# Logarithm and exponential from one named activation table; block inverses with their products in turn at different array positions

## The chip, the cores and the metric

The kernel runs on one core of one Trainium2 chip. A core has five engines that take their instructions from queues of their own: PE (TensorE, the matrix engine), DVE (VectorE), ACT (ScalarE), POOL (GpSimd) and SP (SyncE, which here only starts transfers). They meet through semaphores. PE has a clock that a throttle grants; in the rows it stands at 1.2 GHz (granted clock 0.50) or 2.4 GHz (1.00). The metric is the device time of one execution in microseconds, lower is better: 3612.3 us, the median of three runs (3611.49, 3612.3, 3624.09).

## What is computed

One inference step of a two-layer model over 128 context tokens and 1024 latent tokens of width 1024. Layer 0 mixes tokens by bidirectional gated linear attention (GLA) with pooling, layer 1 by a bidirectional gated delta rule with 8 heads, and each layer ends with a gated feed-forward network with a width-3 convolution. What the change touches, cut from the reference:

```python
def _layernorm(x, g, b):
    ...
    return ((xf - mu) * lax.rsqrt(var + EPS) * g + b)
def _delta_chunk(q, k, v, g, beta, s0):
    ...
    ld = exp(where(incl, b[..., :, None] - b[..., None, :], -inf))
    kk = where(strict, einsum('bhnid,bhnjd->bhnij', kb, k) * ld, 0.0)
    t = triangular_solve(eye + kk, eye, lower=True, unit_diagonal=True)
    u = einsum('bhnij,bhnjv->bhniv', t, v * beta[..., None])
    ...
    def step(s, xs):          # one chunk after the other
        v_new = u_c - w_c @ s
        o = q_c @ s + a_c @ v_new
        s = s * d_c + k_c.T @ v_new
```

So every head needs the inverse of a unit triangular matrix for every chunk, in both directions, before its scan over the chunks can start. Logarithms and exponentials come from the gates (log-sigmoid, softplus, decays) and from every reciprocal square root, which the kernel computes as exp(-0.5 ln x).

## The kernel before, in words

All 1152 tokens stay on the chip in 9 tiles of 128, or 3 chunks of 384 columns. The three-pass products (`L306` to `L308`: high by high, low by high, high by low) are the bulk of PE's work: projections and feed-forward. Other work of PE is laid between them by generators: a line `yield` ends a slot, and `tick` lets the next generator in a list go on by one slot. The order of the instructions is thus fixed when the program is written out; on the chip each engine runs its list in that order.

The activation tables. ACT evaluates Ln, Exp, Silu, Sqrt and others from a table that has to be loaded (`ACT_TABLE_LOAD`). Before the change nothing in the kernel names one; the compiler puts a load ahead of each activation whose function isn't in the table that it takes to be loaded, and it takes Ln and Exp from two different tables. So the reciprocal square root (`rsqrt`, `L315` Ln and `L316` Exp) has a load ahead of each of its two activations. It is used by the layer norms (`lnr<-psvar`) and by the GLA output's norm (`ss`). The GLA gates (`L1063`, `L1064`), the delta heads' preparation (`L1462` Ln of the key norms, `L1466` Exp) and the delta gates (`L1400` to `L1403`) alternate in the same way.

The delta stage. Heads run one after the other. Head h's scan has 9 steps of 3 slots, 27 slots: `L1690` (key by state), `L1706` (query by state) with `L1708` (inverse by residual, reads the tile U), `L1716` (state update) with `L1727` (output). A scan step is a chain of PE, DVE and ACT, so between a scan's slots PE runs one slot of other work: a slot of the output projection (`parts`: three-pass products `L306` to `L308`, or a transpose and two products at `L827`), of the finishing of the head before (`fin`), and of the next head's inverse (`inv`), which begins at slot `ILAG` = 7 and is run for h < 7. Head 0's own inverse runs ahead of its scan, by itself.

The inverse (`inverse`, from `L1605`). The 32 by 32 blocks on the diagonal have been inverted earlier by substitution, in a batch over all heads, and lie in memory as `yd`. For each head and direction the kernel loads them in quarters into T (`T<-yd`, transposed pairs) and U (`U<-yd`), beside the matrix N itself (`Nl<-Nd`). The other blocks follow by products: for each of two directions and two pairs of blocks, XS = N block by T block (`L1615`), U block = -(XS by U block) (`L1625`), and for one pair in each direction a T block = -(U by XS) (`L1632`): ten products of 32 by 32 blocks, each 9 matmuls (one per tile of 128) that all stand at the same position in the PE array. Then the same with 64 by 64 blocks: XH = N by T (`L1643`) and U block = -(XH by U) (`L1653`), eight groups of 5 or 4 matmuls. Each product writes one bank of PSUM, and ACT brings it to SBUF (`L1617` copy, `L1627` and `L1634` times -1). Each product is a slot: 18 slots, at slots 7 to 24 of the scan of the head before.

Banks of PSUM. In the delta stage four banks are in the pool that `self.ps()` takes from in turn, for all but the scan itself (which has pk0, pk1, po0, po1): the three-pass products, the transposes at `L827` and the inverse share them.

Loads. SP issues all transfers of this stage from one list, in the order in which the slots ask for them: `Nl`, then T, then U, `vt`, `ktok`, between the scan's `qka` tiles. Each issue sits behind the issue before it.

Of the kernel before, what the change touches and what calls it, by code (L numbers as in the profile page):

```python
# [19 lines left out]
T = TC + TL  # L20
# [235 lines left out]
class Kern:  # L256
    def __init__(self, tc, I, O):
        self.tc, self.nc, self.I, self.O = tc, tc.nc, I, O
        self.bg, self.side, self.sums = [], [], {}
        self.pe = ExitStack()  # L260

        self.pace = 0

# [45 lines left out]

    def rsqrt(self, out, in_, scale, tmp=None):  # L310
# [4 lines left out]
        nc.scalar.activation(t, in_, AF.Ln, bias=self.eps[:n], scale=scale)  # L315
        nc.scalar.activation(out, t, AF.Exp, scale=-0.5)  # L316
# [64 lines left out]
    def consts(self):  # L381
# [7 lines left out]
        nc.scalar.activation(self.sc32[:, :, 0:2], self.cc, AF.Silu)  # L389
# [267 lines left out]
    def ffn(self, l, lnp, last, order):  # L657
# [21 lines left out]
        def gate(f, t, raws, dst):  # L679

            n = 1153
            for i in (1, 0):
# [6 lines left out]
                if i:  # L689
                    nc.scalar.activation(t[1], t[1], AF.Silu)  # L690
# [21 lines left out]
        def gate_t(c, f, pss, t, hh, hl):  # L712
# [4 lines left out]
            for i in (1, 0):  # L717
# [11 lines left out]
                if i:  # L729
                    nc.scalar.activation(t[1], t[1], AF.Silu)  # L730
# [205 lines left out]
    def in_proj0(self, p, vp):  # L936
# [9 lines left out]
        with L("pool0") as pp:  # L946
# [16 lines left out]
            with L("rgate") as rp:  # L963
                rt = {}
    
                def evac_r(b, c, ps):
# [4 lines left out]
                    if c == NC - 1:  # L971
                        nc.scalar.activation(rt[b], rt[b], AF.Silu)
# [62 lines left out]
    def gla_a(self, hb, p):  # L1035
# [47 lines left out]
        for d in range(2):  # L1083
# [4 lines left out]
            nc.scalar.activation(x, b, AF.Exp)  # L1088
            nc.vector.tensor_tensor(tiles(y), last.to_broadcast([128, NT, 128]), tiles(b), op=ALU.subtract)
            nc.scalar.activation(y, y, AF.Exp)  # L1090
# [19 lines left out]
        def decays(s):  # L1110
# [10 lines left out]
            nc.scalar.activation(e, e, AF.Exp)  # L1121
# [254 lines left out]
    def silu(self, out, x):  # L1376
        self.nc.scalar.activation(out, x, AF.Silu)
# [7 lines left out]
    def gates_body(self, p):  # L1385
# [14 lines left out]
        nc.scalar.activation(l, l, AF.Exp, scale=-1.0)  # L1400
        nc.scalar.activation(l, l, AF.Ln, bias=1.0)
        al = p.tile([128, 16], F32, name="al")
        nc.scalar.activation(al, self.v("a_log"), AF.Exp)  # L1403
# [14 lines left out]
        nc.scalar.activation(self.negeb, self.b, AF.Exp)  # L1418
        nc.vector.tensor_scalar(self.negeb, self.negeb, -1.0, None, op0=ALU.mult)
        ptv = pt[:, :NT * 16].rearrange("p (n h) -> p n h", h=16)  # L1420
        nc.scalar.activation(self.dec, ptv, AF.Exp)
# [14 lines left out]
    def delta_a(self, h, qT, kT, tp):  # L1436
# [25 lines left out]
        nc.scalar.activation(ss, ss, AF.Ln, bias=self.eps)  # L1462
# [3 lines left out]
        nc.scalar.activation(kl, ss, AF.Exp, scale=0.5)  # L1466
# [4 lines left out]
        nc.scalar.activation(rho, rho, AF.Exp)  # L1471

        flat = lambda t: t.rearrange("p n i -> p (n i)")
        for d, t in ((0, Nt[1]), (1, At[1])):
            x = flat(t)
            nc.scalar.activation(x, bc[:, d], AF.Exp)  # L1476
# [6 lines left out]
        for d in range(2):  # L1483
            c = 8 * d + h
            for n in range(NT):
                e = bc[:, d, n * 128:n * 128 + 128]
                nc.vector.scalar_tensor_tensor(e, e, self.b[:, n, c:c + 1], self.v("msk_b" if d else "msk_f"), op0=ALU.subtract, op1=ALU.min)  # L1487
                nc.scalar.activation(e, e, AF.Exp, bias=lrho[:, d, n:n + 1])
# [116 lines left out]
    def inverse(self, N, Us, T64, tp):  # L1605
# [345 lines left out]
```

## Time and profile before

| | us |
|---|---|
| median of three runs | 3612.3 (3611.49, 3612.3, 3624.09) |
| the profiled execution | 3613.56 |
| its span (first to last instruction) | 3611.7 |
| PE busy | 3278.3 (91%) |
| DVE busy | 2264.6 (63%) |
| POOL busy | 1189.1 (33%) |
| ACT busy | 1145.0 (32%) |
| delta heads, first scan to end of the last | 2203.5 to 2607.6 |

The span is what the profile resolves; 1.9 us of the profiled execution lie around it. A busy share is a mean over stages. PE is busy in nearly all of the feed-forward stages; in the delta stage it is filled by the slots described above; it stands still at the ends of stages, where a norm or a gate has to be finished first. What ended last is read from the chain of waits, which goes back from the last instruction to what released each one.

### The profile page before, as it was taken

The page shows a single profiled execution, that of the slowest core. Times are in us where ns is not written, and L with a number is a line of the kernel's source. Part 1 is how long each engine was busy: PE and PEld are TensorE (multiplying, and loading weights), DVE is VectorE, ACT ScalarE, POOL GpSimd, SP SyncE. Part 2 cuts the span into 40 slices and gives each one's busy share as a digit, 9 for nine tenths or more (in the row PEclk, how much of TensorE's full clock was granted, in tenths as well). Part 3 has the DMA queues.
Part 4 walks back from the last instruction along what each step waited for, and adds up shares of the span by engine and source line. Part 5 has one row for each costly group of instructions (what it writes and reads, how often), then busy time and mean ns, then how long its engine had stood idle before and what let it go on. Part 6 is the DMA issues. An engine that isn't in the chain of part 4 may idle for free.

```text
span 3611.7 us, 54689 instructions
## 1 busy us (share of the span) xinstructions
PE 3278.3 (91%) x21774; PEld 3050.6 (84%) x21774; DVE 2264.6 (63%) x3749; ACT 1145.0 (32%) x2334; POOL 1189.1 (33%) x768
## 2 busy tenths in 40 slices
PE   6988898999999999789789899899969999999887
PEld 4877677899999989688778888799858999999886
DVE  4386465656665677664577774655646667576766
ACT  2434323511111111455343432455563111111133
POOL 1221136322222325543223330344533232222454
PEclk9989878999999999889889997899979999999998
DMA  6212544122222112214544647554401111111232
GB/s 253 93 60 77 166 142 135 67 91 100 88 94 82 47 40 84 82 59 137 165 150 154 198 145 222 161 152 152 135 18 40 37 47 42 41 42 41 65 99 93
DMA packets 248877, 370.18 MB, mean 102 GB/s; under 512 B 67647, under 2 KB 185695, under 8 KB 248240
## 3 DMA queue, kind: packets, MB, share of 16 engines
q1 hardware_dynamic: 240612, 349.54, 30.2%
q10 hardware_dynamic: 7340, 14.92, 1.2%
q8 instruction: 173, 2.83, 0.3%
q0 software_dynamic: 672, 2.23, 0.2%
q14 instruction: 80, 0.66, 0.1%
HBM read 284.69 MB, written 81.93 MB: 102 GB/s over the span
## 4 chain that ended last, share of the span: by engine, by line
PE 66%; DVE 17%; ACT 7%; DMA 5%; issue 2%; SPq 1%; POOL 1%; ACTq 0%; DVEq 0%; POOLq 0%
PE ps L306 18%; PE ps L307 17%; PE ps L308 17%; DVE bc L1487 2%; DVE S L513 2%; DVE lns L522 2%; PE psm L419 1%; DVE lnt L572 1%; DVE S L584 1%; DVE cv L728 1%; DMA bc<-brow 1%; ACT UH L612 1%; ACT lnt L614 1%; PE po L1727 1%; PE pk L1716 1%
## 5 line engine op out<-in xcount | busy, mean ns | idle before, releaser
L306 PE MATMUL ps<-UH,whi 128*128 128x384 f32 (+1 forms) x3408 | 1212.0, 356 | 9.3 <-ACT UH L612 7.3
L307 PE MATMUL ps<-UL,whi 128*128 128x384 f32 (+1 forms) x3408 | 1174.6, 345 | 33.6 <-POOL UL L589 23.9
L308 PE MATMUL ps<-UH,wlo 128*128 128x384 f32 (+1 forms) x3408 | 1170.9, 344 | 3.9 <-POOL wlo L245 3.9
L513 DVE SCALAR_TENSOR_TENSOR S<-ps,mod,S 128x384 f32<-128x384 f32 (+1 forms) x1376 | 603.4, 507 | 479.1 <-PE ps L308 478.8
L244 POOL TENSOR_SCALAR whi<-raw 128x1024 fp32r<-128x1024 f32 x262 | 306.9, 1171 | 1705.6 <-PE ps L307 1164.1
L306 PEld LDWEIGHTS ps<-UH,whi 128*128 128x128 f32 x3408 | 659.8, 194 | 63.8 <-issue 43.8
L307 PEld LDWEIGHTS ps<-UL,whi 128*128 128x128 f32 x3408 | 660.9, 194 | 44.0 <-POOL UL L589 26.9
L245 POOL TENSOR_TENSOR wlo<-raw,whi 128x1024 fp32r<-128x1024 f32 x262 | 660.4, 2521 | 21.9
L308 PEld LDWEIGHTS ps<-UH,wlo 128*128 128x128 f32 x3408 | 659.5, 194 | 4.8 <-POOL wlo L245 4.8
L306 PE MATMUL ps<-hh,whi 128*128 128x384 f32 x1056 | 367.1, 348 | 43.0 <-DVE S L513 17.9
L308 PE MATMUL ps<-hh,wlo 128*128 128x384 f32 x1056 | 363.0, 344 | 4.0 <-POOL wlo L245 4.0
L307 PE MATMUL ps<-hl,whi 128*128 128x384 f32 x1056 | 361.0, 342 | 0.3 <-DVE hl L733 0.3
L306 PEld LDWEIGHTS ps<-hh,whi 128*128 128x128 f32 x1056 | 202.7, 192 | 54.6 <-issue 25.8
L690 ACT ACTIVATE cv<-cv 128x1153 f32<-128x1153 f32 x36 | 42.2, 1173 | 616.9 <-DVE cv L687 616.9
L687 DVE SCALAR_TENSOR_TENSOR cv<-raw,vec,cv 128x1153 f32<-128x1153 f32 x136 | 204.6, 1504 | 4.6
L308 PEld LDWEIGHTS ps<-hh,wlo 128*128 128x128 f32 x1056 | 202.8, 192 | 4.6 <-POOL wlo L245 4.6
L307 PEld LDWEIGHTS ps<-hl,whi 128*128 128x128 f32 x1056 | 203.3, 193 | 1.1 <-DVE hl L733 1.1
L651 ACT COPY raw<-ps 128x384 f32<-128x384 f32 (+2 forms) x272 | 94.9, 407 | 344.7 <-PE ps L308 344.7
L516 POOL TENSOR_TENSOR S<-S,gp 128x384 f32<-128x384 f32 x96 | 97.0, 1013 | 173.5 <-ACT gp L511 173.0
L684 DVE TENSOR_SCALAR cv<-raw,vec 128x1153 f32<-128x1153 f32 x68 | 112.8, 1658 | 13.5 <-ACT raw L651 13.5
L728 DVE SCALAR_TENSOR_TENSOR cv<-ps,vec,cv 128x383 f32<-128x383 f32 (+4 forms) x128 | 61.6, 513 | 83.1 <-ACT edge L724 63.3
L1487 DVE SCALAR_TENSOR_TENSOR bc<-bc,bsum,vecd 128x128 f32<-128x128 f32 x144 | 97.6, 746 | 20.3 <-ACT NA L1476 20.3
(316 smaller groups left out, 4239.2 us busy)
## 6 DMA issues: line engine op xcount, KB each, us to landing
raw<-wall SPq DMA_DIRECT2D x260, 512.0 KB
qka<-pack SPq DMA_DIRECT2D x144, 192.0 KB
lnt<-wmod SPq DMA_DIRECT2D x48, 512.0 KB
wm<-wmod SPq DMA_DIRECT2D x40, 512.0 KB
pack<-NA SPq DMA_DIRECT2D x32, 576.0 KB
bc<-brow SPq DMA_DIRECT2D x16, 576.0 KB
Nd<-NA SPq DMA_DIRECT2D x16, 576.0 KB
pack<-cv SPq DMA_DIRECT2D x16, 512.0 KB
```

The lines of the kernel that those rows point to most:

```text
L244: nc.gpsimd.tensor_scalar(hi, raw, 1.0, 0.0, op0=ALU.mult, op1=ALU.add)
L245: nc.gpsimd.tensor_tensor(lo, raw, hi.bitcast(F32), op=ALU.subtract)
L306: mm(out, wh, uh, start=first, stop=False)
L307: mm(out, wh, ul, start=False, stop=False)
L308: mm(out, wl, uh, start=False, stop=last)
L513: nc.vector.scalar_tensor_tensor(d, ps[:, lo - c * CW:hi - c * CW], g, d, op0=ALU.mult, op1=ALU.add)
L516: nc.gpsimd.tensor_tensor(d, d, t, op=ALU.add)
L651: nc.scalar.copy(raw[:, d:d + hi - lo], ps[:, lo - c * CW:hi - c * CW])
L684: nc.vector.tensor_scalar(t[i], raws[i][:, 0:n], w[:, 0:1], None, op0=ALU.mult)
L687: nc.vector.scalar_tensor_tensor(t[i], raws[i][:, k:n + k], w[:, k:k + 1], t[i], op0=ALU.mult, op1=ALU.add)
L728: nc.vector.scalar_tensor_tensor(t[i][:, a:b], ps[:, a + o:b + o], w[:, k:k + 1], t[i][:, a:b], op0=ALU.mult, op1=ALU.add)
L1487: nc.vector.scalar_tensor_tensor(e, e, self.b[:, n, c:c + 1], self.v("msk_b" if d else "msk_f"), op0=ALU.subtract, op1=ALU.min)
```

## The change

Two things. First, a method `act` replaces `nc.scalar.activation` wherever the function is Ln, Exp, Silu or Sqrt. It keeps the name of the table set that it loaded last; if the function belongs to another set, it loads that set by name. Ln and Exp both belong to `natural_log_exp_and_others`. Activations with other functions (copy, square, abs, scaling) are as before. Second, `inverse` computes the same 18 products in 7 bursts: the four XS products together, one matmul of each in turn, at four different array positions, then the four U products, the two T products, and the 64-wide products of the two directions in pairs. Each product still has a bank of its own, so the first two bursts hold four banks at once. The evacuations follow each burst. Behind every burst stand two `yield`s, so a burst is issued at every other slot: slots 7, 9, 11, 13, 15, 17 and 19.

```diff
         self.pace = 0
+        self.tables = None
...
 
+    def act(self, out, in_, func, **k):
+
+        s = {AF.Silu: "silu_and_others", AF.Sqrt: "sqrt_and_others"}.get(func, "natural_log_exp_and_others")
+        if s != self.tables:
+            self.nc.scalar.preload_act_table_set(s)
+            self.tables = s
+        self.nc.scalar.activation(out, in_, func, **k)
+
     def rsqrt(self, out, in_, scale, tmp=None):
 
         nc = self.nc
         t = out if tmp is None else tmp
         n = in_.shape[0]
-        nc.scalar.activation(t, in_, AF.Ln, bias=self.eps[:n], scale=scale)
-        nc.scalar.activation(out, t, AF.Exp, scale=-0.5)
+        self.act(t, in_, AF.Ln, bias=self.eps[:n], scale=scale)
+        self.act(out, t, AF.Exp, scale=-0.5)
...
             x = g[:, n0:n1]
-            nc.scalar.activation(x, x, AF.Exp, scale=-1.0)
-            nc.scalar.activation(x, x, AF.Ln, bias=1.0)
+            self.act(x, x, AF.Exp, scale=-1.0)
+            self.act(x, x, AF.Ln, bias=1.0)
...
-        self.nc.scalar.activation(out, x, AF.Silu)
+        self.act(out, x, AF.Silu)
...
         pairs = [((0, 1), (2, 3)), ((3, 2), (1, 0))]
-        for d in range(2):
-            for a, b in pairs[d]:
-                ps = self.ps()
-                for n in range(NT):
-                    nc.tensor.matmul(ps[qd(b), 32 * n:32 * n + 32], N[d][qd(a), n, qd(b)], T64[d][qd(a), n, 32 * (a % 2):32 * (a % 2) + 32],
-                                     start=True, stop=True, tile_position=(32 * a, 32 * b))
-                nc.scalar.copy(XS[qd(b), d], ps[qd(b), :288].rearrange("p (n c) -> p n c", c=32))
-                yield
-        for i in range(2):
-            for d in range(2):
-                a, b = pairs[d][i]
-                U, Tt = Us[d], T64[d]
-                ps = self.ps()
-                for n in range(NT):
-                    nc.tensor.matmul(ps[qd(a), 32 * n:32 * n + 32], XS[qd(b), d, n], U[qd(b), n, qd(b)],
-                                     start=True, stop=True, tile_position=(32 * b, 32 * a))
-                nc.scalar.mul(U[qd(a), :, qd(b)], ps[qd(a), :288].rearrange("p (n c) -> p n c", c=32), -1.0)
-                yield
-                if i == 0:
-                    ps = self.ps()
-                    for n in range(NT):
-                        nc.tensor.matmul(ps[qd(b), 32 * n:32 * n + 32], U[qd(b), n, qd(b)], XS[qd(b), d, n],
-                                         start=True, stop=True, tile_position=(32 * b, 32 * b))
-                    nc.scalar.mul(Tt[qd(b), :, 32 * (a % 2):32 * (a % 2) + 32], ps[qd(b), :288].rearrange("p (n c) -> p n c", c=32), -1.0)
-                    yield
+        cols = lambda ps, x, n: ps[qd(x), 32 * n:32 * n + 32]
+        all9 = lambda ps, x: ps[qd(x), :288].rearrange("p (n c) -> p n c", c=32)
+        half = lambda T, x: slice(32 * (x % 2), 32 * (x % 2) + 32)
+
+        four = [(d, a, b) for d in range(2) for a, b in pairs[d]]
+        pss = [self.ps() for _ in four]
+        for n in range(NT):
+            for ps, (d, a, b) in zip(pss, four):
+                nc.tensor.matmul(cols(ps, b, n), N[d][qd(a), n, qd(b)], T64[d][qd(a), n, half(T64, a)],
+                                 start=True, stop=True, tile_position=(32 * a, 32 * b))
+        for ps, (d, a, b) in zip(pss, four):
+            nc.scalar.copy(XS[qd(b), d], all9(ps, b))
+        yield
+        yield
+        pss = [self.ps() for _ in four]
+        for n in range(NT):
+            for ps, (d, a, b) in zip(pss, four):
+                nc.tensor.matmul(cols(ps, a, n), XS[qd(b), d, n], Us[d][qd(b), n, qd(b)],
+                                 start=True, stop=True, tile_position=(32 * b, 32 * a))
+        for ps, (d, a, b) in zip(pss, four):
+            nc.scalar.mul(Us[d][qd(a), :, qd(b)], all9(ps, a), -1.0)
+        yield
+        yield
+        two = [(d, *pairs[d][0]) for d in range(2)]
+        pss = [self.ps() for _ in two]
+        for n in range(NT):
+            for ps, (d, a, b) in zip(pss, two):
+                nc.tensor.matmul(cols(ps, b, n), Us[d][qd(b), n, qd(b)], XS[qd(b), d, n],
+                                 start=True, stop=True, tile_position=(32 * b, 32 * b))
+        for ps, (d, a, b) in zip(pss, two):
+            nc.scalar.mul(T64[d][qd(b), :, half(T64, a)], all9(ps, b), -1.0)
+        yield
+        yield
         XH = tp.tile([128, NT, 64], F32, name="XH", tag="XH")
         hf = lambda x: slice(64 * x, 64 * x + 64)
-        for d in range(2):
-            a, b = d, 1 - d
+        for second in range(2):
             for n0, n1 in ((0, 5), (5, 9)):
-                ps = self.ps()
+                pss = [self.ps() for _ in range(2)]
                 for n in range(n0, n1):
-                    nc.tensor.matmul(ps[hf(b), 64 * (n - n0):64 * (n - n0) + 64], N[d][hf(a), n, hf(b)], T64[d][hf(a), n, :],
-                                     start=True, stop=True, tile_position=(64 * a, 64 * b))
-                nc.scalar.copy(XH[hf(b), n0:n1], ps[hf(b), :64 * (n1 - n0)].rearrange("p (n c) -> p n c", c=64))
-                yield
-        for d in range(2):
-            a, b = d, 1 - d
-            U = Us[d]
-            for n0, n1 in ((0, 5), (5, 9)):
-                ps = self.ps()
-                for n in range(n0, n1):
-                    nc.tensor.matmul(ps[hf(a), 64 * (n - n0):64 * (n - n0) + 64], XH[hf(b), n], U[hf(b), n, hf(b)],
-                                     start=True, stop=True, tile_position=(64 * b, 64 * a))
-                nc.scalar.mul(U[hf(a), n0:n1, hf(b)], ps[hf(a), :64 * (n1 - n0)].rearrange("p (n c) -> p n c", c=64), -1.0)
+                    c = slice(64 * (n - n0), 64 * (n - n0) + 64)
+                    for d in range(2):
+                        a, b = d, 1 - d
+                        if second:
+                            nc.tensor.matmul(pss[d][hf(a), c], XH[hf(b), n], Us[d][hf(b), n, hf(b)],
+                                             start=True, stop=True, tile_position=(64 * b, 64 * a))
+                        else:
+                            nc.tensor.matmul(pss[d][hf(b), c], N[d][hf(a), n, hf(b)], T64[d][hf(a), n, :],
+                                             start=True, stop=True, tile_position=(64 * a, 64 * b))
+                for d in range(2):
+                    a, b = d, 1 - d
+                    o = a if second else b
+                    u = pss[d][hf(o), :64 * (n1 - n0)].rearrange("p (n c) -> p n c", c=64)
+                    if second:
+                        nc.scalar.mul(Us[d][hf(a), n0:n1, hf(b)], u, -1.0)
+                    else:
+                        nc.scalar.copy(XH[hf(b), n0:n1], u)
+                yield
                 yield
```

At all other places `nc.scalar.activation(...)` or `self.silu` became `self.act(...)` with the same operands. A line number of before grows by 1 from `L306` on, by 9 behind `act`, by 13 at the start of `inverse` and by 21 behind it; every activation that goes through `act` stands at `L317`, and all table loads that remain at `L315`.

The compiled program has 107 table loads before and 55 after; the rest of ACT's list keeps its order. On ACT, at a layer norm at the end (the squares `lnt`, then the reciprocal square root of the variance; `lnr` is its tile, `psvar` the bank with the variance), before:

```order
L559 ACTIVATE lnt<-S 128x768 [waits DVE_49] x4
L315 ACT_TABLE_LOAD
L315 ACTIVATE lnr<-psvar,eps 128x384 [waits PE_49]
L316 ACT_TABLE_LOAD
L316 ACTIVATE lnr<-lnr 128x384 [waits Activation_49]
```

and after the change, on the same engine at the same place:

```order
L568 ACTIVATE lnt<-S 128x768 [waits DVE_49] x4
L315 ACT_TABLE_LOAD
L317 ACTIVATE lnr<-psvar,eps 128x384 [waits PE_49]
L317 ACTIVATE lnr<-lnr 128x384 [waits Activation_49]
```

The load ahead of the logarithm stands as before; the one between logarithm and exponential is gone.

On PE, in head 3's scan at slots 7 to 9, where the inverse of head 4 begins (T0, T1 and U10, U11 are the tiles T and U of the two directions, ps are banks, the DMAHW names are the lanes on which loads report), before:

```order
L1615 MATMUL ps_20670<-T0_17597,Nl_20513 32x32 [waits DMAHW2_49,DMAHW0_49]
L1615 MATMUL ps_20670<-T0_17597,Nl_20513 32x32 x8
L306 MATMUL ps_20681<-ohi_20049,whi_18690 128x384
L307 MATMUL ps_20681<-olo_20050,whi_18690 128x384
L308 MATMUL ps_20681<-ohi_20049,wlo_18691 128x384
L1716 MATMUL pk_20633<-y_20663,kr_20640 128x128 [waits Activation_49]
L1716 MATMUL pk_20634<-y_20665,kr_20645 128x128 [waits DVE_49,Activation_49]
L1727 MATMUL po_20635<-y_20663,qka_20492 128x128
L1727 MATMUL po_20636<-y_20665,qka_20494 128x128
L1615 MATMUL ps_20702<-T0_17597,Nl_20513 32x32 [waits DMAHW0_49]
L1615 MATMUL ps_20702<-T0_17597,Nl_20513 32x32 x8
```

and after, the first round of the first burst and what follows it up to the first round of the second:

```order
L1628 MATMUL ps_20718<-T0_17644,Nl_20561 32x32 [waits DMAHW2_49,DMAHW0_49]
L1628 MATMUL ps_20719<-T0_17644,Nl_20561 32x32 [waits DMAHW0_49]
L1628 MATMUL ps_20720<-T1_17645,Nl_20562 32x32 [waits DMAHW3_49,DMAHW1_49]
L1628 MATMUL ps_20721<-T1_17645,Nl_20562 32x32 [waits DMAHW1_49,Activation_49]
...
L307 MATMUL ps_20762<-ohi_20152,whi_18782 128x384 [waits Activation_49]
L1737 MATMUL pk_20681<-y_20711,kr_20688 128x128
L307 MATMUL ps_20783<-ohi_20152,whi_18782 128x384 [waits Activation_49]
L1711 MATMUL pk_20790<-Sd_20768,qka_20598 128x128 [waits DMAHW6_49,DVE_49]
L1637 MATMUL ps_20806<-U10_17642,XS_20717 32x32 [waits DMAHW7_49,Activation_49]
L1637 MATMUL ps_20807<-U10_17642,XS_20717 32x32 [waits DMAHW1_49,Activation_49]
L1637 MATMUL ps_20808<-U11_17643,XS_20717 32x32 [waits DMAHW6_49]
L1637 MATMUL ps_20809<-U11_17643,XS_20717 32x32 [waits DMAHW2_49,Activation_49]
```

The waits for the four loads of T, which before stood at slots 7 to 10 (`L1615`), now stand at the head of slot 7; the waits for U, before at slots 11 to 16, stand at slot 9; and the first three-pass product behind each burst of four (`L307` here) waits for ACT to empty a bank, which before it didn't. The order of SP's list of transfers is the same before and after.

## Rows read from the trace of the kernel before

**Rows 1.** The page: span, PE and ACT busy, the chain's shares by engine.
```profile
span 3611.7 us, 54689 instructions
...
PE 3278.3 (91%) x21774; PEld 3050.6 (84%) x21774; DVE 2264.6 (63%) x3749; ACT 1145.0 (32%) x2334; POOL 1189.1 (33%) x768
...
PE 66%; DVE 17%; ACT 7%; DMA 5%; issue 2%; SPq 1%; POOL 1%; ACTq 0%; DVEq 0%; POOLq 0%
```

**Rows 2.** Groups of ACT's instructions: line, count | busy us, mean ns | idle before.
```profile
L316 ACT ACT_TABLE_LOAD x21 | 26.9, 1283 | 0.4
```

**Rows 3.** The chain of waits, four places: start us, us, what.
```profile
157.96 0.32 PE ps L307
...
159.89 0.18 PE ps L306
...
494.85 1.28 ACT L316
...
3599.87 1.28 ACT L316
```

**Rows 4.** PE's waits, 130 to 300 us: us in total, times, longest.
```profile
PE ps L1076 <- DVE eqk L1065: 3.4, 3, 2.5
```

**Rows 5.** Timeline of ACT in the GLA output: start us, us, instruction, [idle before].
```profile
445.48 1.28 ACT L315 ACT_TABLE_LOAD   x1
446.77 0.30 ACT L315 ACTIVATE ss<-ss,eps 128x4 f32<-128x4 f32 x1
```

**Rows 6.** Timeline of PE while head 3 scans, with head 4's inverse.
```profile
2429.36 0.61 PE L1727 MATMUL po<-y,qka 128*128 128x128 f32 x4
2429.72 0.42 PE L306 MATMUL ps<-ohi,whi 128*128 128x384 f32 x1
...
2436.02 0.75 PE L1708 MATMUL pk<-r,U 128*128 128x128 f32 x4 [0.20 <-DVE r L1692]
2436.92 0.72 PE L1615 MATMUL ps<-T,Nl 32*32 32x32 f32 x18 [0.16 <-DMA T<-yd]
...
2438.65 0.61 PE L1727 MATMUL po<-y,qka 128*128 128x128 f32 x4
2439.19 0.75 PE L1615 MATMUL ps<-T,Nl 32*32 32x32 f32 x18
2439.87 0.44 PE L306 MATMUL ps<-ohi,whi 128*128 128x384 f32 x1
...
2442.10 0.61 PE L1706 MATMUL po<-Sd,qka 128*128 128x128 f32 x4
...
2457.77 0.79 PE L1643 MATMUL ps<-T,Nl 64*64 64x64 f32 x10
```

**Rows 7.** Timeline of PE in GLA: products whose matmuls alternate between array positions.
```profile
214.07 0.82 PE L1133 MATMUL ps<-eqk 64*32 64x32 f32 x72
...
250.93 0.80 PE L1175 MATMUL ps<-eqk 64*64 64x64 f32 x20
```

**Rows 8.** Timeline of SP's queue: start of the issues, us that they take together.
```profile
2434.76 3.20 SPq L1582 DMA_DIRECT2D T<-yd  x4
...
2444.06 0.92 SPq L1592 DMA_DIRECT2D U<-yd  x2
```

**Rows 9.** The chain of waits again, transfers in the delta stage.
```profile
2220.56 3.04 DMA U<-yd
...
2434.76 2.17 DMA T<-yd
```

**Rows 10.** Timeline of PE while head 1 scans.
```profile
2273.19 1.14 PE L1615 MATMUL ps<-T,Nl 32*32 32x32 f32 x18 [2.45 <-DMA T<-yd]
```

**Rows 11.** Busy time by stretch; the figure behind the engines is the granted clock.
```profile
2400.00:2600.00 200.00, 198.57 (x1970) 184.49 (x1969) 111.44 (x319) 107.13 (x312) 88.04 (x78) 1.00 0.51 158
...
2272.20:2302.90 30.70, 28.50 (x233) 26.18 (x234) 11.64 (x30) 9.63 (x26) 9.55 (x8) 0.50 0.47 135
```

**Rows 12.** Groups of ACT's instructions: the first evacuations of the inverse.
```profile
L1617 ACT COPY XS<-ps 32x288 f32<-32x288 f32 x32 | 12.5, 390 | 18.5 <-PE ps L1615 18.3
```

More of the change, by code (lines that the diff above doesn't have):

```diff
@@ L388, in consts @@
         nc.vector.memset(self.sc32, 0.0)
-        nc.scalar.activation(self.sc32[:, :, 0:2], self.cc, AF.Silu)
+        self.act(self.sc32[:, :, 0:2], self.cc, AF.Silu)
         self.mod = cp.tile([128, DEPTH, 6, KB, 2], F32, name="mod")
@@ L689, in gate @@
                 if i:
-                    nc.scalar.activation(t[1], t[1], AF.Silu)
+                    self.act(t[1], t[1], AF.Silu)
             h = t[0]
@@ L729, in gate_t @@
                 if i:
-                    nc.scalar.activation(t[1], t[1], AF.Silu)
+                    self.act(t[1], t[1], AF.Silu)
             nc.vector.tensor_tensor(t[0], t[0], t[1], op=ALU.mult)
@@ L971, in evac_r @@
                     if c == NC - 1:
-                        nc.scalar.activation(rt[b], rt[b], AF.Silu)
+                        self.act(rt[b], rt[b], AF.Silu)
                         nc.sync.dma_start(self.sr[b], rt[b])
@@ L1120, in decays @@
             nc.vector.tensor_tensor(k4[:, :, 1], rb, bb[:, :, 1], op=ALU.subtract)
-            nc.scalar.activation(e, e, AF.Exp)
+            self.act(e, e, AF.Exp)
             return e
@@ L1399, in gates_body @@
         nc.scalar.activation(l, ab, AF.Abs)
-        nc.scalar.activation(l, l, AF.Exp, scale=-1.0)
-        nc.scalar.activation(l, l, AF.Ln, bias=1.0)
+        self.act(l, l, AF.Exp, scale=-1.0)
+        self.act(l, l, AF.Ln, bias=1.0)
         al = p.tile([128, 16], F32, name="al")
-        nc.scalar.activation(al, self.v("a_log"), AF.Exp)
+        self.act(al, self.v("a_log"), AF.Exp)
         g = p.tile([128, NT, 16], F32, name="g")
@@ L1470, in delta_a @@
             nc.vector.tensor_tensor(rho[:, d], lrho[:, d], self.kdl[:, :, c], op=ALU.add)
-        nc.scalar.activation(rho, rho, AF.Exp)
+        self.act(rho, rho, AF.Exp)
         flat = lambda t: t.rearrange("p n i -> p (n i)")
@@ L1475, in delta_a @@
             x = flat(t)
-            nc.scalar.activation(x, bc[:, d], AF.Exp)
+            self.act(x, bc[:, d], AF.Exp)
             for a in (0, TC):
@@ L1487, in delta_a @@
                 nc.vector.scalar_tensor_tensor(e, e, self.b[:, n, c:c + 1], self.v("msk_b" if d else "msk_f"), op0=ALU.subtract, op1=ALU.min)
-                nc.scalar.activation(e, e, AF.Exp, bias=lrho[:, d, n:n + 1])
+                self.act(e, e, AF.Exp, bias=lrho[:, d, n:n + 1])
                 if n % 3 == 2:
@@ L1750, in delta_finish @@
         nc.vector.tensor_tensor(ss, ss, rq, op=ALU.mult)
-        nc.scalar.activation(ss, ss, AF.Sqrt, bias=self.eps, scale=1.0 / 128)
+        self.act(ss, ss, AF.Sqrt, bias=self.eps, scale=1.0 / 128)
         yield
@@ L1811, in lengths @@
                 rq = self.rq.rearrange("p h n -> p (h n)")
-                nc.scalar.activation(rq, ps[:, :72], AF.Sqrt, bias=self.eps)
+                self.act(rq, ps[:, :72], AF.Sqrt, bias=self.eps)
                 nc.vector.reciprocal(rq, rq)
```

12 lines of the change are left out of this document (6 added, 6 removed).

## The prediction

> **What bounds the kernel now.** I read the page first [rows 1]: PE is busy for 3278.3 of 3611.7 us, ACT for 1145.0, and 66% of the chain of waits are PE's, 7% ACT's. So what shortens ACT counts only where ACT is in the chain, and what shortens PE counts only where PE isn't going to wait for something else instead. Next I read ACT's groups [rows 2] for what a table load costs, then the chain at each place where a load stands in it [rows 3], PE's waits in the GLA stage [rows 4] and ACT's timeline around a load [rows 5]. For the second half I read PE's timeline through one delta head [rows 6], the products that already alternate between array positions in GLA [rows 7], SP's queue beside that head [rows 8], the chain's transfers [rows 9], a head in which PE waits for its loads [rows 10], and the granted clock by stretch [rows 11].
>
> **The table loads.** The change takes 52 of 107 loads out. Each takes 1.283 us [rows 2], so ACT's busy time falls by 52 x 1.283 = 67 us. Most of that is beside other work. Where a load stood in the chain, its 1.28 us are the chain's: by my count of the chain 16 of the removed loads stand in it, the last of them at 3599.87 [rows 3], at most 16 x 1.28 = 20.5 us. They fall into three kinds.
> - At the ends of stages, where nothing else can go on. Two loads stand at the GLA output's last norm (one is the row at 494.85), eight in layer norms, delta heads and the tails, the last at 3599.87 [rows 3]. A layer norm has had its first load early, while it waited for the variance; the second, between logarithm and exponential, is what goes. Ten loads, 12.8 us; I take 10.5, since behind a few of them a transfer or POOL is nearly as late.
> - In the GLA gates, six in the chain, 7.7 us. What PE there really lost is 3.4 us in three waits for DVE, which waits for ACT [rows 4], so I take 3.5.
> - All others, in the GLA output but for its last chunk, and in the preparation of the delta heads, lie under PE's three-pass products. Nothing, and if that cover went, 1.28 us each.
> Together -14 us, between -5 (only half of the ends) and -21 (all).
>
> The row at 445.48 shows what surrounds a load: it runs 1.28 us, and the activation behind it starts 0.01 us after its end [rows 5]. The Trainium skill's page "ScalarE: Activation LUTs", section "What ACT_TABLE_LOAD costs", gives about 1.28 us for the load and about 1.38 more for a drain, 2.66 for a switch. The load agrees, the drain doesn't show in this trace; with it the term of 14 us would be an estimated 29. I go by the row.
>
> **The inverse on PE.** A product has a price of its own and one for entering its mode. Alone at one position its 18 matmul records (two per product of f32) last until the next instruction starts, 2439.87 - 2439.19 = 0.68 us. In front of it the four `L1727` take 2439.19 - 2438.65 = 0.54, where ahead of a three-pass product they take 2429.72 - 2429.36 = 0.36 [rows 6]; so 0.18 for the entry, and 0.86 for a slot. A 64-wide group of 10 takes 0.79 as shown, 0.07 less to the next start (as 0.75 is to 0.68), 0.72, and 0.90 with the entry [rows 6]; the group of 8 by its share 0.58 + 0.18 = 0.76. The inverse before: 10 x 0.86 + 4 x 0.90 + 4 x 0.76 = 15.2 us for each of the seven heads that host one.
> No trace shows the new bursts, but GLA has products of the same make: 72 records over four positions in 0.82, and 20 over two in 0.80 [rows 7], less 0.07 each. With an entry that gives 0.93 for each of the two bursts of 72, 0.91 for 20, 0.76 for 16; the burst of 36 I put at one product's 0.86. After: 2 x 0.93 + 0.86 + 2 x 0.91 + 2 x 0.76 = 6.1 us. So 9.1 us less of PE's time per head, 64 for seven. That is the most it can bring; the other end is the case where nothing overlaps (a rival below).
>
> **What is late next: the loads.** The first burst needs all of T and N at slot 7, where before the last quarter was needed at slot 10; the second needs U at slot 9, before at 11 to 16. SP's list hasn't changed. In head 3's scan the last of the four T issues starts about 2434.76 + 3 x 0.80 = 2437.2 [rows 8]. From issue to landing a quarter takes 2.17 to 3.04 [rows 9]: 2439.3 to 2440.2. PE is there at 2436.92, and even waits 0.16 for its first quarter [rows 6]. So the first burst waits 2.4 to 3.3 us. Behind it on PE stand the whole scan and the projection; all wait. The last U that the second burst needs is the first of the pair issued at 2444.06 [rows 8], landing at 2446.2 to 2447.1. PE gets there earlier: from 2436.92 to the scan's `L1706` at 2442.10 are 5.18 us, of which three products are 2.6; so 2.6 of other work lie between, and with the first burst (2440.0 + 0.93), most of that work and a wait for a bank it arrives at about 2443.8 and waits 2.4 to 3.3 again. The `L1706` of slot 10 then comes at 2446.7 + 0.93 + the rest of its slot (0.6) + a bank (0.4) = 2448.6 instead of 2442.10: 6.5 us behind. From there on the old inverse had 15.2 - 2.6 = 12.6 us to come, the new 6.1 - 1.9 = 4.2: 8.4 us ahead. Net -1.9 us for such a head.
> The bank wait comes from four banks being held at once: an evacuation takes 0.39 us [rows 12], so a burst of 0.93 leaves four of them, 1.56 us, and the next product waits for the first. The page "TensorEngine Tiling (Array Packing)" of the Trainium skill, section "PSUM Bottleneck", says that behind a fourfold speedup of TensorE the emptying of PSUM may become the limit. The rows agree in size; as a price it is 0.4 to 0.6 us at two places in a head, already counted above.
>
> **Two more costs.** The inverse's products were also the cover under which DVE and ACT did the scan's own steps. Eleven slots of each head lose theirs; an uncovered slot waits up to 0.20 us for DVE's residual [rows 6]. 0 to 2.2, I take 1.0.
> The clock: after PE's wait of 2.45 us in head 1 [rows 10] the granted clock stood at 0.50 from 2272.2 to 2302.9, against 1.00 in heads 3 to 6 [rows 11]. In GLA, after a wait of similar length, three-pass products of 0.32 us turn to 0.18 again some 4 us later [rows 3]. The first costs about 15 us, the second about 2. New waits of this length come into heads 2 to 6, so the price is 0 to +15 for each; I take +1, near the GLA row, since the first wait's slow stretch runs out under the second wait.
> Steady heads (3 to 6): -1.9 + 1.0 + 1 = 0. Heads 0 to 2 already wait for these loads in part [rows 10], so there the saved work is worth more: -0.9 - 2.45 = -3.4 each, without a clock term, since two of them are at the lower level anyway: -10. Head 0's own inverse ahead of its scan gets shorter too, but it waits for U, then the scan for its reloaded N: 0. Inverse together: -10, between -28 (the shorter landing times, no clock price, no uncovered latency) and +10 (longer landings and 2 to 3 us of clock in each).
>
> **Sum.** 3613.6 - 14 - 10 = 3589.6 against the profiled execution, which is 1.3 above the median: 3588 us.
>
> **Rivals.**
> - The loads come in time (SP's queue slides forward with a quicker head, or the lanes are free earlier). Then the whole of the inverse counts: 64 - 7 x 1.0 = 57, with the tables 71: 3541. For it: the transfer alone is only 2.17 to 3.04. Against it: SP issues the T quarters at 0.80 each behind `Nl`, whose place is set by the head's start, and nothing moves that. 0.08.
> - The inverse gives nothing or a little less than nothing, and the tables half of their term: 3600 to 3612, say 3606. For it: every one of the loads at the stage ends has POOL, DVE and transfers beside it, and the steady heads come out at 0 already. Against it: the two loads at 493 and those at the tail have nothing beside them. 0.22.
> - Slower: each of the two waits brings PE to its lower clock and it stays there for the rest of the inverse, as in head 1 [rows 10, 11]. Price about 15 us in each of heads 3 to 6 and 5 in head 2, +65, less 14 and less 10: 3653; it turns the sum against the change from about 6 us in each of the five heads (24 / 5, and the 1 already counted). For it: that row. Against it: bursts are fewer and shorter, so more of what follows is three-pass products. 0.07.
> The Trainium skill's page "TensorE: Matmul & The Clock Gate", section "Why this matters for your kernels", advises against idle gaps between bursts of matmuls, for the throughput drops. It speaks for this rival; the trace shows both a long and a short drop.
> - The change doesn't do what it says: matmuls of 32 by 32 at four positions don't overlap. Then a burst of 72 takes four times 0.5 us and more, only the entries are saved (11 x 0.18 = 2 us per head), and the waits of 6.5 remain: +4 in each of seven heads, +28, less 14: 3626. Against it: 72 records in 0.82 [rows 7]. 0.04.
>
> **How the numbers follow.** The forecast has 0.59, with 3573 to 3605 as its own range. The range of 3556 to 3616 takes in the forecast and the second rival and leaves out the first and the two slower ones, 0.19. 0.5% is 18 us, about what a measurement of this kernel can tell from no change: faster is below 3594. The forecast lies below it in about 7 of 10 of its cases (0.41), with the first rival 0.08 and a little of the second 0.04: 0.53. Slower: the last two, 0.11. The rest, 0.36, is within.
>
> **What would show it.** In the trace after: ACT busy near 1078 us and 55 loads; no load between `lnr`'s two activations; one wait for `T<-yd` and one for `U<-yd` in every hosting head, 2.4 to 3.3 us each, on the first matmuls of the two bursts; bursts of 72 in about 0.8 us; a wait of the three-pass product behind them for ACT; hosting heads still 47 to 50 us apart in heads 3 to 6; the granted clock near 0.9 there. Heads of 40 us would prove the loads wrong, heads of 55 the clock, bursts of 2 us the overlap. The sum would be wrong in its first term if the stretches at 493, 2688, 2726 and 3562 keep their length.

## The result and the profile after

The changed kernel takes 3562.73 us (median of 3563.03, 3553.43, 3579.48 and 3562.42), the kernel before 3611.89. The ratio is 0.9878 with an interval of 0.984 to 0.9917, so 44 us faster (30 to 58). The forecast was 3588, 24 us faster, with a range of 3556 to 3616: right in direction and inside the range, but little more than half the size.

The page after shows the change done. Its span, its busy times and the shares of the chain of waits:

```profile
span 3561.0 us, 54650 instructions
...
PE 3194.8 (90%) x21774; PEld 2979.9 (84%) x21774; DVE 2269.7 (64%) x3749; ACT 1082.2 (30%) x2282; POOL 1187.6 (33%) x768
...
PE 64%; DVE 18%; ACT 7%; DMA 7%; issue 2%; SPq 1%; POOL 1%; ACTq 0%; DVEq 0%; POOLq 0%
```

Against [rows 1], ACT has 52 instructions and 63 us less, PE the same number of instructions and 84 us less, and DMA's share of the chain has risen from 5% to 7%: the first sign of the waits for loads. The table loads, from the groups of ACT's instructions:

```profile
L315 ACT ACT_TABLE_LOAD x55 | 70.6, 1283 | 1.7 <-PEq L1965 0.7
```

The last of them in time, from ACT's timeline at the end; it answers to the row at 3599.87 in [rows 3]:

```profile
3545.17 1.28 ACT L315 ACT_TABLE_LOAD   x1
3549.77 0.58 ACT L317 ACTIVATE lnr<-psvar,eps 128x384 f32<-128x384 f32 x1 [3.32 <-PE psvar L578]
3550.38 0.52 ACT L317 ACTIVATE lnr<-lnr 128x384 f32<-128x384 f32 x1
```

The exponential now starts 0.03 us after the logarithm ends; before the change a load of 1.28 us stood between them.

The inverse of head 5 while head 4 scans, from PE's timeline; it answers to [rows 6]. (The text ahead of the result counts that scan as head 3's. Counted from the first scan at 2203.5 it is head 4's; the numbers don't depend on it.)

```profile
2387.58 0.61 PE L1729 MATMUL pk<-vt,U 128*128 128x128 f32 x4
...
2396.38 0.24 PE L1628 MATMUL ps<-T,Nl 32*32 32x32 f32 x2
2397.70 0.24 PE L1628 MATMUL ps<-T,Nl 32*32 32x32 f32 x2 [1.07 <-DMA T<-yd]
2398.75 0.92 PE L1628 MATMUL ps<-T,Nl 32*32 32x32 f32 x68 [0.81 <-DMA T<-yd]
2400.10 0.69 PE L307 MATMUL ps<-ohi,whi 128*128 128x384 f32 x1 [0.44 <-ACT XS L1631]
...
2404.14 0.25 PE L1637 MATMUL ps<-U,XS 32*32 32x32 f32 x4
2406.36 1.11 PE L1637 MATMUL ps<-U,XS 32*32 32x32 f32 x68 [1.96 <-DMA U<-yd]
2408.00 0.87 PE L836 MATMUL ps<-vec,od 128*128 128x128 f32 x3 [0.53 <-ACT U L1640]
2408.66 1.06 PE L1727 MATMUL po<-Sd,qka 128*128 128x128 f32 x4
...
2411.61 0.76 PE L1647 MATMUL ps<-XS,U 32*32 32x32 f32 x36
2414.65 0.80 PE L1666 MATMUL ps<-T,Nl 64*64 64x64 f32 x20
```

Read it from the top. The first burst gets its first products at once and waits twice for T, 1.88 us in all. Four banks are then full, and the projection waits 0.44 for ACT. The second burst waits 1.96 for U. In heads 3 to 6 the waits for T add up to 2.6, 1.9, 2.5 and 1.9 us, those for U to 2.0, 2.0, 2.8 and 1.0. `L1727` of slot 10 comes 21.1 us after the head's start; in [rows 6] it came 2442.10 - 2427.61 = 14.5 after it (2427.61 is the first `L1708` of that scan). So the head is 6.6 behind there; 6.5 was forecast. That the two figures are so close is partly luck: both waits of this head are below the 2.4 to 3.3 us that were forecast, and work at half clock makes up for it. From 2400.1 to 2403.2 the granted clock is 0.50, by an estimate half of these 3.1 us, and the forecast had put the clock into a term of its own. Then the bursts pay it back, and the head takes 47.7 us (2387.58 to 2435.3) where it took 49.0.

Where the 50.8 us between the two profiled executions lie follows from lining them up by SP's transfers, which stand in the same order in both: the start of the same transfer in both traces, stretch by stretch.

| stretch (times of before) | change, us | forecast |
|---|---|---|
| to 399, GLA | +2.5 | -3.5 |
| 399 to 739, GLA output and first projection | -15.4 | -2.5 |
| 739 to 2206, feed-forward, norms, delta preparation | -9.4 | part of the -8 below |
| head 0 | -12.0 | -3.4 |
| heads 1 to 6 | -6.7 | -6.8 |
| behind the heads, to the end | -9.8 | -8, with the row at 739 |

In sum heads 1 to 6 came out as worked out. One by one they didn't: head 1 -3.7, head 2 -1.4, heads 3 to 6 together -1.4, where -3.4, -3.4 and 0 were forecast. Three terms are larger: the GLA output, head 0 and the ends. The GLA stage came out with the other sign.

### The profile page after: what moved, and what is told of

Read it like the earlier page. It is cut to its first block, busy times and chain, and to the rows that moved or that the text cites. A ratio compares the mean times of both kernels' runs of the same rounds, so it can differ in the third digit from the quotient of the medians.

```text
span 3561.0 us, 54650 instructions
## 1 busy us (share of the span) xinstructions
PE 3194.8 (90%) x21774; PEld 2979.9 (84%) x21774; DVE 2269.7 (64%) x3749; ACT 1082.2 (30%) x2282; POOL 1187.6 (33%) x768
## 4 chain that ended last, share of the span: by engine, by line
PE 64%; DVE 18%; ACT 7%; DMA 7%; issue 2%; SPq 1%; POOL 1%; ACTq 0%; DVEq 0%; POOLq 0%
PE ps L307 18%; PE ps L308 17%; PE ps L309 17%; DVE bc L1496 2%; DVE S L522 2%; DVE lns L531 2%; PE psm L428 1%; DVE lnt L581 1%; DVE cv L737 1%; DVE S L593 1%; ACT UH L621 1%; DMA Nl<-Nd 1%; ACT lnt L623 1%; DVE tY L1564 1%; PE ps L836 1%
## 5 line engine op out<-in xcount | busy, mean ns | idle before, releaser
L307 PE MATMUL ps<-UH,whi 128*128 128x384 f32 (+1 forms) x3408 | 1210.7, 355 | 8.8 <-ACT UH L621 5.3
L307 PEld LDWEIGHTS ps<-UH,whi 128*128 128x128 f32 x3408 | 660.0, 194 | 64.7 <-issue 46.0
L307 PE MATMUL ps<-hh,whi 128*128 128x384 f32 x1056 | 366.5, 347 | 44.3 <-DVE S L522 20.0
L317 ACT ACTIVATE cv<-cv 128x1153 f32<-128x1153 f32 (+1 forms) x84 | 82.9, 987 | 769.4 <-DVE cv L696 617.0
L307 PEld LDWEIGHTS ps<-hh,whi 128*128 128x128 f32 x1056 | 202.5, 192 | 56.2 <-issue 29.1
```

The costliest lines, as they stand in the source:

```text
L307: mm(out, wh, uh, start=first, stop=False)
```

## The experiments

Each ran on a chip with runs of the kernel before beside it. One kernel's executions spread widely here, those of the kernel before in one session from 3586 to 3622, so a ratio with its interval is worth more than one time, and a difference between two traces is not yet an effect of the edit. The run of the inverse alone and the repeats below show how much that matters.

**The table half alone** (the method `act` and all its calls; the old `inverse`).

> The kernel before with the first half of the change alone: the method act and the named table set; the inverse as before. Theory A (tables worth more than predicted): lined up by their transfers, the two traces part by 13 us in the GLA output and by some 18 us in the rest outside the delta heads, so the time is 3612 - 31 = 3581. Theory B (the 13 us in the GLA output are a chance of the clock, which turned 25 us later in the one profiled execution; tables worth what the prediction said, 14 to 18): 3594 to 3598. In the trace: by A the GLA output (stretch from the last kdl transfer to the start of the feed-forward) keeps the higher clock into its second half, by B it falls at some other time than in the trace of the whole change.

3568.77 us on six runs, ratio 0.9888 (0.9848 to 0.9927). Repeated at the end, unchanged:

> The table half alone once more, unchanged, since its two parts by themselves gave 1 and 12 us and the whole 38 on six runs. Theory A (the table half's own worth is the sum of its steps outside the GLA output, 17 to 20 us, and the GLA output's 12 to 14 us come or don't come by chance, whatever is done to the loads): a median between 3578 and 3592, below it where the GLA output is short in most runs; the steps at the layer norms and the tail as in its first trace within 2 us. Theory B (the two parts only work together): 3569 again within 5 us, and the GLA output short in the trace. Theory C (its worth is the 13 us of the two parts): 3592 or more.

3587.68 on eight runs, ratio 0.9933 (0.9905 to 0.9961). That is 40 us (26 to 55) and 24 (14 to 34). In the first trace 14.2 of 34.4 us lie in the GLA output (434 to 469 in times of before) and 3.6 in heads 0 and 1, whose inverse this kernel doesn't touch; in the second, of 48.3 us, 12.6 and 19.8. What is left is 17 and 16 us.

**The inverse alone** (the new `inverse`, no `act`).

> The kernel before with the second half alone: the inverse in seven bursts; all 107 table loads stay. Theory A: the heads give what they gave in the whole change, 12 in head 0, 4 in head 1, 3 over the other five: 3612 - 19 = 3593. Theory B: the inverse is worth more and the tables less, since the sum was measured at 49: 3612 - 49 + 16 = 3579. In the trace: heads 3 to 6 47.5 to 50 us apart by both, a wait for T and one for U in each; head 0 43 us by A, 55 if its gain came from the tables.

3592.51, ratio 0.9964 (0.9942 to 0.9986): 13 us (5 to 21), as theory A had it. Heads 3 to 6 take 48.0 to 48.9 us, head 0 42.8.

**Both kernels again**, unchanged, for a second trace each.

> The kernel before once more, unchanged, for a second trace. Theory A (chance decides in the GLA output): the granted clock may fall at another place than 20 us into that stretch. Theory B (the table loads decide): it falls within 20 to 26 us again, and the stretch takes as long as before within 3 us.

> The changed kernel once more, unchanged. Theory A: the GLA output's clock falls at any place between 20 and 50 us into the stretch. Theory B: past 40 us, as in its first trace. Steady heads by both: 47.5 to 50 us apart; each layer norm's end 1.3 us shorter for each load taken out of it.

3588.57 and 3571.98 us, one run each. The kernel before now had its head 0 in 39.4 us instead of 55.1, without any edit. The changed kernel had the GLA output as long as the kernel before. Both of the large terms move by themselves. In the rows of busy time by stretch the third figure from the end is the granted clock. The GLA output from 28 to 40 us into it, kernel before, first and second trace:

```profile
426.70:438.70 12.00, 12.00 (x50) 7.82 (x49) 4.40 (x8) 7.28 (x11) 1.49 (x2) 0.50 0.80 268
```
```profile
424.90:436.90 12.00, 12.00 (x50) 7.77 (x49) 4.46 (x8) 7.28 (x11) 0.75 (x1) 0.50 0.84 284
```

and the changed kernel, first and second trace:

```profile
429.20:441.20 12.00, 12.00 (x81) 8.56 (x79) 7.40 (x14) 5.76 (x14) 1.50 (x2) 1.00 0.97 331
```
```profile
428.50:440.50 12.00, 12.00 (x50) 8.29 (x49) 3.89 (x7) 2.79 (x7) 0.99 (x1) 0.50 0.83 260
```

PE is busy for all of the 12 us in each, and gets 81 matmuls done at 1.00 and 50 at 0.50. Head 0, kernel before, first and second trace, and the changed kernel:

```profile
2203.50:2258.60 55.10, 52.92 (x422) 46.81 (x422) 29.88 (x95) 17.92 (x55) 0.00 (x0) 0.66 0.61 182
```
```profile
2197.10:2236.50 39.40, 38.49 (x423) 34.44 (x422) 28.62 (x95) 17.54 (x55) 0.00 (x0) 0.92 0.83 254
```
```profile
2181.20:2224.20 43.00, 33.35 (x423) 29.36 (x422) 28.19 (x95) 18.02 (x56) 0.00 (x0) 0.84 0.84 248
```

With the old inverse at slot 7, seven traces of head 0 show 55.1, 39.4, 54.1, 55.9, 55.1, 55.1 and 39.5 us; with the bursts at slot 7, four show 43.0, 42.7, 42.8 and 45.6. In none of these four is the long case seen; against the short one the bursts cost 3 to 6 us. The means differ by 7 us. Head 1 swings as well, from 58.8 to 68.0 us with the old inverse, and lies at 60.7 to 61.1 with the bursts; the means of heads 1 and 2 differ by 3.2 and 3.5 us, those of heads 3 to 6 by 0.7 each. So the bursts at slot 7 shorten the seven heads by some 17 us, of which 7 are head 0's.

**Loads put back in the GLA output** (whole change):

```diff
-                self.rsqrt(ss, ss, 1.0 / 128)
+                nc.scalar.preload_act_table_set("natural_log")
+                nc.scalar.activation(ss, ss, AF.Ln, bias=self.eps, scale=1.0 / 128)
+                nc.scalar.preload_act_table_set("exp_and_others")
+                nc.scalar.activation(ss, ss, AF.Exp, scale=-0.5)
+                self.tables = "exp_and_others"
```

> The whole change with 19 table loads put back at one place: the reciprocal square root of the GLA output's norm loads the logarithm's and the exponential's table by itself, as before, nine times each. Theory A (these loads bring PE to its lower clock early in the GLA output and cost 13 us): 3563 + 13 = 3576 or more, with the clock falling in the first third of that stretch. Theory B (only the last chunk's two loads are exposed): 3563 + 2.6 = 3566, with the clock's fall at any place.

3576.17, ratio 0.9915 (0.9885 to 0.9945), not apart from the whole change by its interval. The median is the one that theory A named, but in the trace the clock held until some 50 us into the stretch with the old loads in place. That speaks against A's mechanism, by which these loads make it fall early.

**Transfers moved in the GLA output** (kernel before):

```diff
         mq = [self.mods([(0, 4)], p, 2, dma=nc.scalar)]
-        self.tick(1, mq)
...
         for n in range(3):
             ahead(n)
+        self.tick(1, mq)
```

> The kernel before, with one thing moved: in the GLA output the first two transfers of 512 KB for the modulation (wm) start behind the state pass instead of ahead of it. No table load and no part of the inverse is changed. Theory A (the clock there is decided by how long PE waits for the kdl and Al transfers some 20 us into that stretch, not by ACT's tables): the waits for kdl fall from 5.3 us in total to about 3, the clock stays at its upper level past 40 us into the stretch, and the stretch is 10 to 14 us shorter, as in three of the four runs with the new tables. Theory B (the table loads decide it): waits change, the clock falls about 20 to 25 us in as in the kernel before, and the time is within 3 us of it.

3609.05, ratio 0.998 (0.9954 to 1.0006). The clock dipped for some 5 us, 15 us into the stretch, came back and fell for good behind 30 us instead of 20, and the time didn't move: neither theory, and no lever found.

**The table half in two parts** (old inverse; the flag is off up to the end of the GLA output and then on for the GLA part, the other way round for the rest):

```diff
+        if self.split and func in (AF.Ln, AF.Exp):
+            s = "natural_log" if func == AF.Ln else "exp_and_others"
         if s != self.tables:
```

> The kernel before with the shared table up to the end of the GLA output alone; from there on logarithm and exponential load a table each, as before (26 of the 52 loads are gone). The table half as a whole was worth 38 us in its medians, though the steps of its trace outside the GLA output add up to 20. Theory A (the loads taken out of the GLA stage make it likelier that the clock holds in the GLA output, which is worth 12 to 14 us, and they give 3 to 5 us by themselves): 15 to 20 us below the kernel before. Theory B (the GLA output's clock is chance alone and the 38 us come from stage ends): within 6 us of it.

> The other part: the shared table from the end of the GLA output on alone, with the GLA stage's loads as before (27 loads are gone). Theory A: 17 to 20 us below the kernel before, the sum of the steps that the trace of the whole table half shows at the layer norms, in the delta stage's preparation and at the tail; in the GLA output the clock falls 20 to 30 us into the stretch, as in all traces with the old loads there. Theory B: 32 us or more below it.

GLA part 3606.35, ratio 0.9995 (0.9969 to 1.0022); the rest 3595.41, ratio 0.9963 (0.9939 to 0.9987), 13 us (5 to 22). Their traces have 82 and 81 loads, so 25 and 26 of the 52 are gone, one less in each than the expectations count. In the GLA output the first was slow with the new loads, the second quick with the old ones:

```profile
423.50:435.50 12.00, 12.00 (x50) 8.31 (x52) 3.91 (x7) 2.79 (x7) 0.82 (x1) 0.50 0.83 256
```
```profile
427.60:439.60 12.00, 11.52 (x78) 8.13 (x76) 6.61 (x12) 10.06 (x18) 1.90 (x2) 1.00 1.06 351
```

Over the fourteen traces the clock held in that stretch in three of seven with GLA's loads gone and in two of seven with them. So no link of the GLA output's clock with the table loads is shown. But the two parts add up to 15 us, each with a margin of some 9; the whole gave 40 and 24, of which only the second has 15 in its interval. What makes the difference stays open.

**A later start of the inverse** (whole change, one constant; in the other run 10):

```diff
-ILAG = 7
+ILAG = 13
```

> The whole change with the inverse begun at slot 13 of the scan instead of slot 7 (one constant), so that the first burst comes about 17 us behind the head's start and the second about 20, behind the landings of T (13 us) and U (19 us). Theory A (the waits for these loads take back what the bursts save): no wait for T or U is left, heads 3 to 6 fall from 48.5 to 42 or 43 us, and seven heads give 35 us: 3563 - 35 = 3528. Theory B (the scan's own chain through DVE and ACT takes their place, or the clock stays): heads stay over 46 us and the time over 3550.

> The whole change with the inverse begun at slot 10, between 7 and 13. By the loads' landings (13 us behind a head's start for T, 19 for U) the first burst, at about 13.5 us, waits no more than 0.5, the second, at 16, still waits 2 to 3. Theory A (each wait is paid by itself): heads 3 to 6 at 45 to 46 us, between 48.5 and 42.4, and a time of 3563 - 16 = 3547. Theory B (one wait is enough to bring the lower clock and the whole price): heads at 48 us, the time over 3557.

At 13: 3531.99, ratio 0.9794 (0.9764 to 0.9824), the fastest kernel of this study, 74 us below the kernel before. At 10: 3548.82, ratio 0.9824 (0.979 to 0.9859). Heads 3 to 6 took 43.2, 41.8, 42.6, 41.9 at slot 13 and 46.4, 44.7, 47.4, 44.9 at slot 10. PE's timeline in head 4 at slot 13:

```profile
2389.06 0.82 PE L1628 MATMUL ps<-T,Nl 32*32 32x32 f32 x72
2390.32 0.44 PE L307 MATMUL ps<-ohi,whi 128*128 128x384 f32 x1 [0.44 <-ACT XS L1631]
...
2392.90 1.11 PE L1637 MATMUL ps<-U,XS 32*32 32x32 f32 x72
2394.46 0.44 PE L307 MATMUL ps<-ohi,whi 128*128 128x384 f32 x1 [0.45 <-ACT U L1640]
```

No wait for T or U is left, in heads 3 to 6 not one; the two waits for a bank are. At slot 10 the first burst goes through and the second still waits:

```profile
2402.33 0.97 PE L1628 MATMUL ps<-T,Nl 32*32 32x32 f32 x72
...
2406.00 0.25 PE L1637 MATMUL ps<-U,XS 32*32 32x32 f32 x4
2408.43 0.89 PE L1637 MATMUL ps<-U,XS 32*32 32x32 f32 x68 [2.18 <-DMA U<-yd]
```

Busy time and clock of head 4's scan in the changed kernel and at slot 13:

```profile
2387.60:2435.30 47.70, 42.82 (x503) 40.57 (x502) 26.11 (x77) 26.25 (x76) 20.48 (x19) 0.93 0.55 165
```
```profile
2372.10:2413.90 41.80, 40.22 (x503) 37.63 (x502) 24.86 (x76) 25.77 (x76) 20.43 (x19) 1.00 0.62 188
```

Of the 5.9 us between them, PE's busy time gives 2.6 (the clock) and its idle time 4.9 - 1.6 = 3.3 (the waits). Each wait is paid by itself, as theory A had it.

The control, the kernel before with `ILAG = 9`:

> The kernel before with its inverse begun at slot 9 instead of 7, the latest start at which its 18 slots end with the scan. It is the control for the run with the bursts at slot 13. Theory A (a later start helps only where PE waited for the loads): the waits for T and U in heads 0 and 1, 10 us in all, go, heads 3 to 6 stay at 49, and the time falls by 5 to 12 us. Theory B (the later start by itself is most of the gain of the run at slot 13): 20 us or more.

3607.68, ratio 0.9986 (0.9968 to 1.0005), 5 us at best estimate; heads 3 to 6 at 48.4 and 48.5, where the seven traces at slot 7 have 48.9 on average. A later start does next to nothing for steady heads whose inverse doesn't wait. The gain at slot 13 is that of the bursts, once the loads are there.

## Why the prediction was right or wrong

- **The loads of the next head eat most of what the bursts save.** Right, and shown: the two waits, the delay behind them, heads 3 to 6 nearly unchanged (0 forecast; -0.5, -1.2, +1.5, -1.2 in the trace, -0.7 each over the eleven traces), the inverse 10 us forecast and 13 (5 to 21) measured alone. With the loads out of the way heads fall by 6 us. That the delay is 6.6 against 6.5 is partly luck, as said above, and the 10 against 13 hide that head 0 gave 7 on average where 3.4 were forecast. The first rival was the right picture of what is under the waits, in a kernel that starts the inverse later.
- **The bursts themselves.** 0.93 us for 72 records forecast; 0.82 and 1.11 shown for the two bursts at slot 13. The next instruction waits for a bank, 0.44 to 0.53 against the 0.4 to 0.6 forecast. The rival in which positions don't overlap is out.
- **The clock.** +1 us per head was taken. Behind each of the two waits PE runs some 3 us at half its clock: a three-pass product behind the first burst lasts 0.69 where it lasts 0.42 undisturbed ([rows 6], at 2429.72). The granted clock of the head is 0.93, near the 0.9 named. The slower rival, a whole head at half clock, didn't come.
- **The table term was mis-sized.** -14 was forecast, -5 to -21 allowed. Alone it measured 40 us (26 to 55) and, repeated, 24 (14 to 34). The failed step is the count that put ten loads at the ends at 10.5 us, 8 of them outside the GLA output.

  Over all fourteen traces these ends are worth some 16: the stretch behind the heads is 0.4 us shorter to 3.9 longer than in the first trace where its old loads stand (six traces) and 4.0 to 11.8 shorter where they are gone (eight), 10 us between the means; from 739 to 2206 the means are 5 us apart, though the two groups overlap. At the GLA output's last norm, where two loads of the chain stand, it is 7.8 us from the end of PE's last product to the start of the transfer behind the norm (`S<-xT`) in all seven traces with these loads and 6.3 in all seven without: 1.6 us for two loads, of the 2.5 forecast.

  The count took its places from the chain of waits, which shows one path. The load at 2649.71 wasn't on it, yet PE waited for what stands behind it, before and after the change:

```profile
2653.31 0.44 PE L306 MATMUL ps<-UH,whi 128*128 128x384 f32 x1 [2.15 <-ACT UH L612]
```
```profile
2608.93 0.44 PE L307 MATMUL ps<-UH,whi 128*128 128x384 f32 x1 [0.86 <-ACT UH L621]
```

  1.29 us, one load exactly, and the product behind it waits 4.66 for POOL in the one and 4.67 in the other, so the gain isn't given back. With such places the steps outside the GLA output and the heads' own swings come to 17 and 16 us in the two traces of the table half alone, above the 14 forecast and inside its bounds. Why the times of that half fell by more than this stays open.
- **The GLA gates**: 3.5 us forecast, +2.5 in the trace, 2 us (-8 to 11) for the GLA part by itself. Over the fourteen traces the means of the stretch to 399 are 1.6 us apart, each with a spread of 7 us or more. Not shown to be worth anything.
- **Head 0 and the GLA output** were each read from one trace, in which both were in their long case. That 15 us and 12 to 14 us come and go there by themselves wasn't in the argument. In the profiled pair they make 23.6 of 50.8 us: 11.6 in the GLA output from 434 to 469, where the forecast had nothing to gain, and 12.0 in head 0. So much of the distance between 24 and 50.8 is chance. What holds over the traces is 17 us in the heads, 16 at the ends, 1.6 at the GLA output's norm and perhaps 2 in the GLA stage, some 36 in all. That lies inside the measured 30 to 58, and above the forecast's 24 mainly by the ends and head 0.
- **The drain of the page "ScalarE: Activation LUTs"** of the Trainium skill (section "What ACT_TABLE_LOAD costs"): its 2.66 us for a switch would have made the term an estimated 29. Taking a load out at 2649.71 gave 1.29. The measurement decides for the load alone there; no run shows what the totals of the table half hold beyond the places named above.

## What to carry to other kernels

When many small products are packed into one burst, all their operands are needed at the time of the first: move the burst behind the last landing before judging it (here 6 us per head, one constant). A load taken out of a serial end can be worth its own length on a path that the profile's chain doesn't follow (here 1.29 us at 2649.71). Take a second trace of the same kernel before a difference between two traces is called an effect: here two stretches swung by 12 to 16 us with no edit.

## What the runs showed of the hardware

With PE busy for 70.0 of 70 us, the granted clock stayed at 0.50 for 70 us in the GLA output (423.7 to 493.7 in the first trace of the kernel before). Being busy did not bring it back in that mix of matmuls, most of them 128 columns wide.

The same wait could be followed by either level. Behind the last wait of the output projection, 2.54 us for `od` in the kernel before and 2.55 in the changed one, the next 11 us ran thus, before and after:

```profile
2630.60:2641.60 11.00, 10.12 (x29) 6.92 (x29) 1.95 (x5) 1.94 (x5) 2.96 (x3) 0.69 0.01 1
```
```profile
2590.30:2601.30 11.00, 9.63 (x39) 6.60 (x38) 4.63 (x9) 3.98 (x8) 3.93 (x4) 1.00 0.00 0
```

Of five traces with all of the old table loads four were at 0.69 or 0.70 there and one, that with the moved transfers, at 1.00; all nine with any of the new loads were at 1.00. That is worth some 2 us, and nothing in the runs says why.
